# Eighteen of twenty-four down-projection blocks per layer by seven block products

## The chip, the cores and the metric

The kernel runs on one core of a Trainium2 chip. The metric is the device time of one execution in microseconds (us). Three runs of the kernel before took 2449.74, 2450.14 and 2452.28 us; the median, 2450.14 us, is the time that the change is measured against. The engines are named as the profile names them: PE (TensorE, matrix products), PEld (its weight loads), DVE (VectorE), ACT (ScalarE), POOL (GpSimd) and SP (SyncE, which here only issues DMAs).

## The reference, cut to what matters

The model is a two-layer decoder trunk on a sequence of 1024 tokens with 1024 features, in float32. Layer 0 mixes tokens by a gated linear recurrence, layer 1 by stick-breaking attention. After each mixer stands a residual sum with layer normalisation, and then the same channel mixer, which is what the change touches:

```
def conv_ffn(x, w_up, conv_w, conv_b, w_down):
    h = causal_depthwise_conv(x @ w_up, conv_w, conv_b)
    return (jax.nn.gelu(h[..., :D_FF]) * h[..., D_FF:]) @ w_down
...
        x = layer_norm(DN_ALPHA * x + mix, ln_g[layer, 0], ln_b[layer, 0])
        f = conv_ffn(x, ffn_w_up[layer], ffn_conv_w[layer], ffn_conv_b[layer], ffn_w_down[layer])
        x = layer_norm(DN_ALPHA * x + f, ln_g[layer, 1], ln_b[layer, 1])
```

D_FF is 3072: `w_up` is 1024x6144 (gate and value halves), `w_down` is 3072x1024. The convolution looks back two tokens.

## The kernel before

Every float32 matrix product is made of three passes: each operand is split into a rounded high part and the rest (`Split`, line 88, `split_sb`: ACT casts the high part, POOL subtracts it from the source for the low part, line 96), and high x high, high x low and low x high are summed in PSUM. A matmul instruction is 128x128 by 128x512.

The channel mixer of a layer has two phases. The **up phase** (`up`, line 421) goes through 24 blocks j of 128 gate and 128 value channels. Blocks 0, 1 and 23 (`PLAIN`) are done plainly, 96 matmuls each (8 slices of 128 features x 2 halves of tokens x 2 operands x 3 passes). The others go through `seven` (line 533): the 2x2 block product of a weight block (gate and value rows by two halves of features) with x (two halves of features by two halves of tokens) is done by seven products of 12 matmuls instead of eight (the Winograd form of Strassen's rule), so 84 matmuls a block. For this DVE makes four sums of weight blocks per block (`combine`, line 459), and the products add up in three PSUM tiles: `p` for one product, and `cv` and `cg`, whose halves are called c21, c22, c11 and c12. Between the products ACT copies c22 to c11 (line 549) and DVE writes c12 = c22 + p (line 554), which must be done before PE may go on adding into c22 in the product called w3 here (its matmuls read `whi` of sum s3). The sums of x that the seven products need (T1 to T4) are made once per layer, in block 0 (`sums_of_x`, line 488), and live in `Ts`.

When a block's products are done, `activate` (line 481) makes the convolution from PSUM (ACT scales, DVE adds two shifted terms, line 477), ACT applies gelu to the gate, DVE multiplies gate by value (line 485), and SP stores the gated block to DRAM (`gd`, 512 KB). With `ug` and `uv` below the gate's and the value's result are meant.

The **down phase** (`down`, line 571) goes through the 24 gated blocks in eight groups of three. `load` brings the three gated blocks and their weight rows back, ACT and POOL split them (128x1024 each), and `accumulate` (line 141) multiplies: per group 8 tiles of 128 tokens x 2 halves of features x 3 blocks x 3 passes = 144 matmuls for 16 PSUM tiles, each added by DVE to the residual `xres` (line 165, line 161 in the first group). The last two groups run with the layer normalisation (`Finish`).

The order on each engine is set by a scheduler when the program is built: each engine takes its own instructions in a fixed order, and waits at each for what it needs. Where two loops meet, a few instructions of the next block stand between those of the last: PE has four matmuls of the next block between the fourth and the fifth product of a block; they are called fillers here. Buffers come from pools (`bufs=` gives how many of a tile there are): a new tile waits until all readers of the tile that had its buffer are done. The pool `sums` has four buffers for the sums s1 to s4.

## Time and profile before

| | |
|---|---|
| median of three runs | 2450.14 us |
| profiled execution | 2452.94 us, of it the span from first to last instruction 2451.2 us |
| PE busy | 2362.0 us, 96% of the span, 10948 matmuls |
| DVE busy | 1330.6 us, 54% |
| POOL busy | 1122.7 us, 46% |
| ACT busy | 926.3 us, 38% |
| granted TensorE clock, mean | 0.983 of full speed |
| DMA | 71 GB/s over the span |

An engine is busy when one of its instructions runs. Matmuls are pipelined, so that each seems to last 389 ns while a new one starts about every 227 ns; PE's pace is read from starts. The stages are: the recurrence up to about 340 us, the up phase of layer 0 to 843, its down phase to 1107, attention to about 1680, the up phase of layer 1 to 2181 and its down phase to the end.

### The profile page before, as it was taken

The page shows a single profiled execution, that of the slowest core. Times are in us where ns is not written, and L with a number is a line of the kernel's source. Part 1 is how long each engine was busy: PE and PEld are TensorE (multiplying, and loading weights), DVE is VectorE, ACT ScalarE, POOL GpSimd, SP SyncE. Part 2 cuts the span into 40 slices and gives each one's busy share as a digit, 9 for nine tenths or more (in the row PEclk, how much of TensorE's full clock was granted, in tenths as well). Part 3 has the DMA queues.
Part 4 walks back from the last instruction along what each step waited for, and adds up shares of the span by engine and source line. Part 5 has one row for each costly group of instructions (what it writes and reads, how often), then busy time and mean ns, then how long its engine had stood idle before and what let it go on. Part 6 is the DMA issues. An engine that isn't in the chain of part 4 may idle for free. (4 is left out here: it accounts for less than half of the span.)

```text
span 2451.2 us, 28627 instructions
## 1 busy us (share of the span) xinstructions
PE 2362.0 (96%) x10948; PEld 1931.2 (79%) x10948; DVE 1330.6 (54%) x1558; ACT 926.3 (38%) x1379; POOL 1122.7 (46%) x776
## 2 busy tenths in 40 slices
PE   8989979999999999999999999988999999999998
PEld 6877768777777888888877887867877777788887
DVE  5695665555555433362565555585655555533336
ACT  4644234444444411113433343343444444431111
POOL 4686265444444553353332232236544444454444
PEclk9999989999999999998999999999999999999999
DMA  6111111222222433202010110001222222153321
GB/s 216 53 54 52 35 43 57 78 82 78 85 88 69 154 112 88 91 12 69 27 35 27 35 35 32 30 18 61 66 90 78 78 82 79 64 180 104 103 69 69
DMA packets 64072, 176.15 MB, mean 72 GB/s; under 512 B 7104, under 2 KB 8768, under 8 KB 63936
## 3 DMA queue, kind: packets, MB, share of 16 engines
q1 hardware_dynamic: 59328, 160.46, 20.4%
q10 hardware_dynamic: 4608, 13.87, 1.7%
q8 instruction: 86, 1.41, 0.2%
q14 instruction: 50, 0.41, 0.1%
HBM read 144.94 MB, written 29.36 MB: 71 GB/s over the span
## 5 line engine op out<-in xcount | busy, mean ns | idle before, releaser
L96 POOL TENSOR_TENSOR wlo<-wraw,whi 128x512 fp32r<-128x512 f32 (+2 forms) x219 | 366.0, 1681 | 436.8 <-ACT whi L90 422.0
L96 POOL TENSOR_TENSOR wlo<-s,whi 128x512 fp32r<-128x512 f32 x168 | 218.0, 1298 | 250.0 <-ACT whi L90 220.0
L165 DVE TENSOR_TENSOR xres<-xres,po 128x512 f32<-128x512 f32 x264 | 169.6, 681 | 294.8 <-PE po L157 294.5
L153 PE MATMUL po<-dh,mh 128*128 128x512 f32 x768 | 299.3, 390 | 0.0
L154 PE MATMUL po<-dl,mh 128*128 128x512 f32 x768 | 298.8, 389 | 0.0
L90 ACT CAST whi<-wraw 128x512 fp32r<-128x512 f32 (+2 forms) x211 | 147.0, 701 | 288.3 <-PE cv L467 134.1
L157 PE MATMUL po<-dh,ml 128*128 128x512 f32 x768 | 237.3, 389 | 0.0
L96 POOL TENSOR_TENSOR ml<-mraw,mh 128x1024 fp32r<-128x1024 f32 x48 | 115.4, 2405 | 231.3 <-ACT mh L90 219.8
L467 PE MATMUL cv<-Th,whi 128*128 128x512 f32 x504 | 205.4, 408 | 1.6
L90 ACT CAST whi<-s 128x512 fp32r<-128x512 f32 x168 | 104.3, 621 | 271.0 <-PE cg L467 145.4
L467 PE MATMUL cv<-Th,wlo 128*128 128x512 f32 x504 | 196.7, 390 | 0.0
L467 PE MATMUL cv<-Tl,whi 128*128 128x512 f32 x504 | 196.6, 390 | 0.0
L153 PEld LDWEIGHTS po<-dh,mh 128*128 128x128 f32 x768 | 144.1, 188 | 30.6 <-DVE xres L165 0.7
L157 PEld LDWEIGHTS po<-dh,ml 128*128 128x128 f32 x768 | 144.2, 188 | 29.9
L154 PEld LDWEIGHTS po<-dl,mh 128*128 128x128 f32 x768 | 144.2, 188 | 29.6
L459 DVE TENSOR_TENSOR s<-wraw 128x512 f32<-128x512 f32 x84 | 60.5, 720 | 188.8 <-POOL wlo L96 188.4
L90 ACT CAST mh<-mraw 128x1024 fp32r<-128x1024 f32 x48 | 50.4, 1049 | 291.3 <-PE po L154 248.5
L114 PE MATMUL pp<-xTh,whi 128*128 128x512 f32 x352 | 143.4, 407 | 1.6 <-ACT whi L90 1.6
L116 PE MATMUL pp<-xTh,wlo 128*128 128x512 f32 x352 | 137.9, 392 | 0.0
L115 PE MATMUL pp<-xTl,whi 128*128 128x512 f32 x352 | 137.7, 391 | 0.0
L467 PEld LDWEIGHTS cv<-Th,whi 128*128 128x128 f32 x504 | 94.4, 187 | 47.4 <-ACT cg L549 17.6
L467 PE MATMUL cg<-xTh,whi 128*128 128x512 f32 x336 | 130.7, 389 | 0.0
(225 smaller groups left out, 5705.0 us busy)
## 6 DMA issues: line engine op xcount, KB each, us to landing
wraw<-in_w_up SPq DMA_DIRECT2D x192, 256.0 KB, 2.7
gd<-u SPq DMA_DIRECT2D x48, 512.0 KB, 3.1
mraw<-gd SPq DMA_DIRECT2D x48, 512.0 KB, 3.6
draw<-in_w_down SPq DMA_DIRECT2D x48, 512.0 KB, 3.9
wraw<-in_w_in SPq DMA_DIRECT2D x14, 512.0 KB, 3.7
wraw<-in_w_o SPq DMA_DIRECT2D x9, 512.0 KB, 3.6
xres<-in_x ACTq DMA_DIRECT2D x8, 512.0 KB, 5.0
wraw<-in_w_out SPq DMA_DIRECT2D x8, 512.0 KB, 3.7
```

What stands on the lines that cost most here:

```text
L90: A.copy(out=hi, in_=src)
L96: eng.tensor_tensor(out=lo, in0=src, in1=hi.bitcast(F32), op=ALU.subtract)
L114: T.matmul(out, lhsT=l.hi, rhs=r.hi, start=start, stop=False)
L115: T.matmul(out, lhsT=l.hi, rhs=r.lo, start=False, stop=False)
L116: T.matmul(out, lhsT=l.lo, rhs=r.hi, start=False, stop=stop)
L153: T.matmul(po[h], lhsT=g.hi, rhs=w.hi[:, d], start=st, stop=False)
L154: T.matmul(po[h], lhsT=g.hi, rhs=w.lo[:, d], start=False, stop=False)
L157: T.matmul(po[h], lhsT=g.lo, rhs=w.hi[:, d], start=False, stop=sp)
L165: V.tensor_tensor(out=xres[t][:, d], in0=xres[t][:, d], in1=po[h], op=ALU.add)
L459: V.tensor_tensor(out=s, in0=x, in1=y, op=op)
L467: T.matmul(ps, lhsT=l, rhs=r[:, c, :], start=start and c == k == 0, stop=stop and c == 3 and k == 2, skip_group_check=True)
```

## The change

The up phase does block 23 by seven products too (`PLAIN` is now blocks 0 and 1). The gated blocks 0 to 17 are taken in nine pairs. For each pair `store` makes, in the up phase of the block after the pair, the four sums of gated half blocks that a seven-product down-projection needs: four instructions on POOL (lines 513 to 519), in buffers of the pool `sums`, and seven DMAs of 256 KB (line 508) in place of two of 512 KB.

In the down phase a new function, `sevens`, does the nine pairs in three groups. A group goes through the seven products one at a time, each over the three pairs: 12 matmuls per pair, 36 per product, into four PSUM tiles of which each is for one tile of 128 tokens in both halves of the sequence. That makes 252 matmuls for the six blocks that took two groups of 144 before. Each product splits its own operands, six of 128x512 (three gated sums, called `graw` when read back, g when split, and three weights, `wr` or `wt`, w when split): ACT casts the high parts, POOL makes the low parts, from the ninth operand on every third of them DVE. The four sums of weights per pair are made on DVE (line 675), three of the four in place. After a product DVE adds its four tiles to `xres`, once or twice (lines 650 and 653). The last six blocks go as before. The four PSUM banks pairs of the down phase are now called px (four banks) and py0, py1 (two each).

Other edits go with these: the raw weight blocks of the up phase have two pools of four buffers instead of one of eight; block j+1's weights are asked for before block j's work; the fourth sum of x (T4) uses the place of a half of x that is not read later, and is made in block 2 instead of block 0, after the second use of c22; `uv` and `ug` have pools of their own; `gap` keeps a place in SBUF free.

```diff
-        PLAIN = (0, 1, NFF - 1)
+        PLAIN = (0, 1)
...
+        NSEV = NFF - 2 * GROUP
+        GAP = GROUP * HS
+
         def ffn(layer, last):
-            gd = [dram.tile([P, S], F32, name=f"gd{layer}_{j}") for j in range(NFF)]
+
+            gd = [[dram.tile([P, HS], F32, name=f"gs{layer}_{m}_{i}") for i in range(7)] for m in range(NSEV // 2)]
+            gd += [dram.tile([P, S], F32, name=f"gd{layer}_{j}") for j in range(NSEV, NFF)]
...
-                rawp = pool("raw", bufs=8)
+                uw = pool("uw", bufs=1)
+                rawp = [pool(f"raw{i}", bufs=4) for i in range(2)]
                 sums = pool("sums", bufs=4)
+                gap = pool("gap", bufs=1)
                 tq = pool("tq", bufs=1)
+
+                gap.tile([P, GAP], F32, name="gap")
...
-                      for i in range(4)]
+                      for i in range(3)] + [xq[0][1]]
...
+                    done.append(ug)
+
+                done = []
+
+                def store(j):
+
+                    if j >= NSEV:
+                        queue = nc.scalar if j == NFF - 1 else nc.sync
+                        queue.dma_start(out=gd[j - NSEV + NSEV // 2], in_=done[j])
+                    elif j % 2:
+                        a11, a21, a12, a22 = two(done[j - 1]) + two(done[j])
+                        s1, s2, s4 = (sums.tile([P, HS], F32, name="s", tag="s") for _ in range(3))
+
+                        def keep(i, x):
+                            nc.sync.dma_start(out=gd[j // 2][i], in_=x)
+
+                        keep(0, a11)
+                        keep(1, a12)
+                        keep(6, a22)
+                        G.tensor_tensor(out=s1, in0=a21, in1=a22, op=ALU.add)
+                        keep(3, s1)
+                        G.tensor_tensor(out=a21, in0=a11, in1=a21, op=ALU.subtract)
+                        keep(4, a21)
+                        G.tensor_tensor(out=s2, in0=s1, in1=a11, op=ALU.subtract)
+                        keep(2, s2)
+                        G.tensor_tensor(out=s4, in0=a12, in1=s2, op=ALU.subtract)
+                        keep(5, s4)
...
+                        if 3 in which:
+                            ts = [None, t2s.pop(0), None, sums.tile([P, HS], F32, name="s", tag="s")]
+                        else:
+                            ts = [sums.tile([P, HS], F32, name="t2" if i == 1 else "s", tag="t2" if i == 1 else "s")
+                                  for i in range(3)] + [None]
+                            t2s.append(ts[1])
+                        for i, p, q in ((0, y[:, lo_], x[:, lo_]), (2, y[:, hi_], y[:, lo_]),
...
                     product(c22, w2, t2, False, False)
+                    if j == len(PLAIN):
+                        sums_of_x((3,))
                     product(c11, w12, b21, False, True)
                     V.tensor_tensor(out=c12, in0=c22, in1=p5s, op=ALU.add)
                     product(c22, w3, t3, False, True)
...
+                    if j:
+                        store(j - 1)
                     activate(j, *ps)
+                store(NFF - 1)
...
+        def sevens(layer, gd, ph, banks):
+            def pool(name, **kw):
+                return ph.enter_context(tc.tile_pool(name=f"{name}_s{layer}", reuse_waits="tile", **kw))
+            wtp = pool("wt", bufs=5)
+            wrps = [None, pool("wr1", bufs=14), pool("wr0", bufs=12)]
+            wrps[0] = wrps.pop()
+            rawp = pool("graw", bufs=4)
+            wfp = pool("wf", bufs=GROUP)
+            ring = pool("ring", bufs=6)
+            def operand(src, name):
+                w = Split(ring.tile([P, HS], F32R, name=name + "h", tag=name + "h"),
+                          ring.tile([P, HS], F32R, name=name + "l", tag=name + "l"))
+                turns[0] += 1
+                split_sb(w.hi, w.lo, src, lo_eng="dve" if turns[0] > 8 and turns[0] % 3 == 0 else "pool")
+                return w
+            turns = [0]
+            seen = set()
+            def add(t, h, ps):
+                x = xres[t][:, HALVES[h]]
+                if (t, h) in seen:
+                    V.tensor_tensor(out=x, in0=x, in1=ps, op=ALU.add)
+                else:
+                    seen.add((t, h))
+                    V.scalar_tensor_tensor(out=x, in0=x, scalar=ALPHA, in1=ps, op0=ALU.mult, op1=ALU.add)
+            for group, m0 in enumerate(range(0, NSEV // 2, GROUP)):
+                B = {}
+                wrp = wrps[group % 2]
+                def weight(n, m):
+                    def w(n):
+                        return weight(n, m)
+                    if (n, m) in B:
+                        return B[n, m]
+                    if n in ("11", "12", "21", "22"):
+                        k, d = int(n[0]) - 1, HALVES[int(n[1]) - 1]
+                        out = (wfp if n == "11" else wrp).tile([P, HS], F32, name="wr", tag="wr")
+                        nc.sync.dma_start(out=out, in_=a["w_down"][layer, (2 * m + k) * P:(2 * m + k + 1) * P, d])
+                    else:
+                        x, y, place = {"T1": ("12", "11", "11"), "T2": ("22", "T1", None), "T3": ("22", "12", "12"),
+                                       "T4": ("21", "T2", "21")}[n]
+                        x, y = w(x), w(y)
+                        out = w(place) if place else wtp.tile([P, HS], F32, name="wt", tag="wt")
+                        V.tensor_tensor(out=out, in0=x, in1=y, op=ALU.subtract)
+                    B[n, m] = out
+                    return out
+                for n in ("11", "21"):
+                    for m in range(m0, m0 + GROUP):
+                        weight(n, m)
+                acc = [None, None]
+                for i, n, c, on, into in ((0, "11", 0, False, ((0, 0),)), (1, "21", 1, False, ((0, 0),)),
+                                          (2, "T2", 0, True, ((0, 1),)), (3, "T1", 1, False, ((1, 1),)),
+                                          (4, "T3", 0, True, ((1, 0), (1, 1))), (5, "22", 1, True, ((0, 1),)),
+                                          (6, "T4", 0, False, ((1, 0),))):
+                    if not on:
+                        acc[c] = [banks[(group + c) % 2].tile([P, HS], F32, name="po", tag="sm") for _ in range(4)]
+                    for m in range(m0, m0 + GROUP):
+                        raw = rawp.tile([P, HS], F32, name="graw", tag="graw")
+                        nc.sync.dma_start(out=raw, in_=gd[m][i])
+                        g = operand(raw, "g")
+                        w = operand(weight(n, m), "w")
+                        for t in range(4):
+                            gt = g[:, t * P:(t + 1) * P]
+                            for k, (l, r) in enumerate(((gt.hi, w.hi), (gt.hi, w.lo), (gt.lo, w.hi))):
+                                T.matmul(acc[c][t], lhsT=l, rhs=r, start=not on and m == m0 and k == 0,
+                                         stop=m == m0 + GROUP - 1 and k == 2, skip_group_check=True)
+                    for t in range(4):
+                        for th, h in into:
+                            add(4 * th + t, h, acc[c][t])
...
+                pends = [pool(f"py{i}", bufs=2, space=PSUM) for i in range(1)]
+                pmid = pool("px", bufs=4, space=PSUM)
+                pends.append(pool("py1", bufs=2, space=PSUM))
+
+                class Ends:
+
+
+                    n = 0
+
+                    def tile(self, *args, **kw):
+                        self.n += 1
+                        return pends[(self.n + 1) // 2 % 2].tile(*args, **kw)
+
+                pend = Ends()
+                with ExitStack() as ph7:
+                    sevens(layer, gd, ph7, (pmid, pend))
...
-                for k in range(NG - 2):
-                    gs, ws = load(k)
-                    accumulate(pb, gs, ws, first=(k == 0))
```

On the engines the change moves instructions at three places. The names carry the program's numbers; the numbers differ between the two programs.

Up phase, DVE, from the gate-times-value product of one block (L485, now L493) to the addition c12 = c22 + p of the next (L554, now L598). Before:

```order
L485 TENSOR_TENSOR u_3178<-u_3178,u_3183 128x1024
L459 TENSOR_TENSOR s_3493<-wraw_3487,wraw_3489 128x512
L554 TENSOR_TENSOR cg_3259<-cv_3233,p5s_3261 128x512
L459 TENSOR_TENSOR s_3495<-s_3493,wraw_3485 128x512
L558 TENSOR_TENSOR cv_3233<-cv_3233,p5s_3261 128x512
```

Now, in the block after a pair:

```order
L485 SCALAR_TENSOR_TENSOR uv_3560<-cv_3462,pv_66,uv_3560 128x1022
L493 TENSOR_TENSOR ug_3555<-ug_3555,uv_3560 128x1024
L467 TENSOR_TENSOR s_3734<-wraw_3567,wraw_3569 128x512
L467 TENSOR_TENSOR s_3736<-s_3734,wraw_3565 128x512
L598 TENSOR_TENSOR cg_3635<-cv_3609,p5s_3637 128x512
L467 TENSOR_TENSOR s_3738<-wraw_3565,wraw_3567 128x512
```

Two sums of the next block's weights stand ahead of the addition instead of one; the second, s_3736, has the buffer of the pair's first gated sum, s_3702 (the pool goes round in four). In the block after that one the addition follows the product directly.

The same place on POOL, after the change (before, there are only instructions of line 96 there):

```order
L96 TENSOR_TENSOR wlo_3743<-wraw_3565,whi_3742 128x512
L513 TENSOR_TENSOR s_3702<-ug_3408,ug_3555 128x512
L515 TENSOR_TENSOR ug_3408<-ug_3408 128x512
L517 TENSOR_TENSOR s_3703<-s_3702,ug_3408 128x512
L519 TENSOR_TENSOR s_3704<-ug_3555,s_3703 128x512
L96 TENSOR_TENSOR wlo_3747<-s_3734,whi_3746 128x512
```

Four sums of gated blocks have moved in ahead of the low part of s_3734; the last reader of s_3702 on POOL is the third of them, and its reader beside POOL is the DMA gs0_2_3 of line 508.

End of the up phase, DVE, from the last block's last addition into c22 (L558 of block 22 before, L602 of block 23 now). Before:

```order
L485 TENSOR_TENSOR u_5990<-u_5990,u_5995 128x1024
L477 SCALAR_TENSOR_TENSOR u_6123<-pg_6026,pv_66,u_6123 128x1023
L477 SCALAR_TENSOR_TENSOR u_6123<-pg_6026,pv_66,u_6123 128x1022
L477 SCALAR_TENSOR_TENSOR u_6128<-pu_6025,pv_66,u_6128 128x1023
L477 SCALAR_TENSOR_TENSOR u_6128<-pu_6025,pv_66,u_6128 128x1022
L161 SCALAR_TENSOR_TENSOR xres0_75<-xres0_75,po_6196 128x512
```

Now:

```order
L602 TENSOR_TENSOR cv_6202<-cv_6202,p5s_6230 128x512
L675 TENSOR_TENSOR wr_6344<-wr_6512,wr_6344 128x512
L675 TENSOR_TENSOR wr_6512<-wr_6510,wr_6512 128x512
L675 TENSOR_TENSOR wr_6346<-wr_6541,wr_6346 128x512
L675 TENSOR_TENSOR wr_6541<-wr_6539,wr_6541 128x512
L485 SCALAR_TENSOR_TENSOR ug_6296<-cg_6228,pv_66,ug_6296 128x1023
L675 TENSOR_TENSOR wt_6515<-wr_6510,wr_6344 128x512
L485 SCALAR_TENSOR_TENSOR ug_6296<-cg_6228,pv_66,ug_6296 128x1022
```

Five sums of down weights have come in ahead of and between the last gate convolution, which frees the PSUM bank that PE's first down matmul writes. Those sums write in place of weights that POOL reads (wl_6367 reads wr_6344, wl_6389 reads wr_6346):

```order
L96 TENSOR_TENSOR gl_6363<-graw_6360,gh_6362 128x512
L96 TENSOR_TENSOR wl_6367<-wr_6344,wh_6366 128x512
L96 TENSOR_TENSOR gl_6385<-graw_6382,gh_6384 128x512
L96 TENSOR_TENSOR wl_6389<-wr_6346,wh_6388 128x512
L96 TENSOR_TENSOR gl_6407<-graw_6404,gh_6406 128x512
L96 TENSOR_TENSOR wl_6411<-wr_6348,wh_6410 128x512
L96 TENSOR_TENSOR gl_6437<-graw_6434,gh_6436 128x512
L96 TENSOR_TENSOR wl_6441<-wr_6350,wh_6440 128x512
```

PE's first down matmuls, right behind block 23, now read gh_6436 with wh_6440 and wl_6441, that is what the seventh and eighth of these instructions write:

```order
L475 MATMUL cv_6202<-xTh01_85,wlo_6199 128x512
L699 MATMUL po_6430<-wh_6440,gh_6436 128x512
L699 MATMUL po_6430<-wl_6441,gh_6436 128x512
L699 MATMUL po_6430<-wh_6440,gl_6437 128x512
```

What moved there: the second product's first tiles stand ahead of the first product; before, the down phase began with the first tile of its first group behind 96 matmuls of block 23.

## Rows read from the trace of the kernel before

**Rows 1.** Stretches: up and down phase, layer 1; length, busy (count) by engine, PEclk.

```profile
1749.00:2151.00 402.00, 401.23 (x1729) 320.99 (x1727) 224.54 (x220) 182.32 (x268) 185.79 (x144) 1.00 0.24 80
2181.00:2443.00 262.00, 261.93 (x1156) 216.56 (x1154) 106.18 (x153) 50.17 (x49) 125.62 (x62) 1.00 0.29 93
```

**Rows 2.** PE's timeline at the start and end of layer 0's down phase.

```profile
842.64 0.61 PE L127 MATMUL pu<-xTh,wlo 128*128 128x512 f32 x2
843.09 0.39 PE L153 MATMUL po<-dh,mh 128*128 128x512 f32 x1
...
1079.73 0.49 PE L230 MATMUL pt<-ident,xres 128*128 128x128 f32 x3
```

**Rows 3.** PE's groups from 843.0 to 1080.0 us.

```profile
L153 PE MATMUL po<-dh,mh 128*128 128x512 f32 x348 | 135.4, 389 | 0.0
```

**Rows 4.** PE's timeline in a block that began at 2101.6: third and fifth product.

```profile
2105.91 0.39 PE L467 MATMUL p<-Th,wlo 128*128 128x512 f32 x1
2106.35 0.50 PE L467 MATMUL cv<-Th,whi 128*128 128x512 f32 x1
...
2112.63 0.39 PE L467 MATMUL cv<-xTh,whi 128*128 128x512 f32 x1
2112.90 0.50 PE L467 MATMUL cv<-Th,whi 128*128 128x512 f32 x1
```

**Rows 5.** DVE's timeline in the same block.

```profile
2101.55 2.60 DVE L477 SCALAR_TENSOR_TENSOR u<-cg,pv,u 128x1023 f32<-128x1023 f32 x2
...
2104.66 2.59 DVE L477 SCALAR_TENSOR_TENSOR u<-cv,pv,u 128x1023 f32<-128x1023 f32 x2
2107.36 2.16 DVE L485 TENSOR_TENSOR u<-u 128x1024 f32<-128x1024 f32 x1
2111.28 0.69 DVE L459 TENSOR_TENSOR s<-wraw 128x512 f32<-128x512 f32 x1 [1.76 <-POOL wlo L96]
2112.15 0.70 DVE L554 TENSOR_TENSOR cg<-cv,p5s 128x512 f32<-128x512 f32 x1 [0.17 <-PE cg L467]
```

**Rows 6.** ACT's timeline in the same block.

```profile
2099.44 1.20 ACT L475 ACTIVATE u<-cg,pv 128x1024 f32<-128x1024 f32 x1
2102.16 1.21 ACT L475 ACTIVATE u<-cv,pv 128x1024 f32<-128x1024 f32 x1
2115.78 0.62 ACT L90 CAST whi<-wraw 128x512 fp32r<-128x512 f32 x1 [3.18 <-PE cv L467]
2116.30 0.58 ACT L557 COPY cv<-cv 128x512 f32<-128x512 f32 x1
```

**Rows 7.** POOL's timeline: four low parts in a row, and two around 398 us.

```profile
359.02 5.02 POOL L96 TENSOR_TENSOR wlo<-wraw,whi 128x512 fp32r<-128x512 f32 x4
...
396.65 2.97 POOL L96 TENSOR_TENSOR wlo<-s,whi 128x512 fp32r<-128x512 f32 x2
```

**Rows 8.** DVE's timeline at 398.4 and 415.3 us.

```profile
398.41 1.76 DVE L459 TENSOR_TENSOR s<-wraw 128x512 f32<-128x512 f32 x1 [0.57 <-POOL wlo L96]
...
415.34 1.23 DVE L485 TENSOR_TENSOR u<-u 128x1024 f32<-128x1024 f32 x1
```

**Rows 9.** The page, DMA issues: KB each, median us from issue to landing.

```profile
wraw<-in_w_up SPq DMA_DIRECT2D x192, 256.0 KB, 2.7
```

**Rows 10.** PE's timeline: first matmul after an idle time (in brackets).

```profile
1395.25 0.62 PE L114 MATMUL pu<-whi,oh 128*128 128x512 f32 x1 [1.80 <-DVE xres L716]
1600.70 0.48 PE L778 MATMUL po<-wth,vh 128*128 128x128 f32 x1 [2.58 <-ACT wth L639]
```

**Rows 11.** Stretches behind such idle times; the third number from the end is PEclk.

```profile
1327.90:1331.30 3.40, 3.06 (x15) 2.31 (x15) 3.40 (x5) 1.15 (x3) 0.45 (x2) 1.00 0.33 135
1395.30:1398.70 3.40, 3.40 (x10) 2.97 (x11) 3.34 (x4) 0.56 (x3) 0.00 (x0) 0.53 0.38 145
1600.80:1604.20 3.40, 3.40 (x10) 2.91 (x11) 2.65 (x6) 1.00 (x3) 0.58 (x2) 0.50 0.00 0
```

**Rows 12.** The page, DVE's additions from PSUM to the residual.

```profile
L165 DVE TENSOR_TENSOR xres<-xres,po 128x512 f32<-128x512 f32 x264 | 169.6, 681 | 294.8 <-PE po L157 294.5
```

More of the change, by code (lines that the diff above doesn't have):

```diff
@@ L452, in blocks @@
                     for f, k in ((0, 0), (1, 0), (1, 1), (0, 1)):
[L453 removed]
+                        raw = out[f, k] = rawp[j % 2].tile([P, HS], F32, name="wraw", tag="wraw")
                         nc.sync.dma_start(out=raw, in_=a["w_up"][layer, f * NFF + j][:, k * HS:(k + 1) * HS])
@@ L481, in activate, with sums_of_x @@
                 def activate(j, pg, pu):
-                    ug = conv(pg, j)
+                    ug = conv(pg, j, "ug", 2)
                     A.activation(out=ug, in_=ug, func=AF.Gelu_apprx_tanh)
-                    uv = conv(pu, NFF + j)
+                    uv = conv(pu, NFF + j, "uv", 1)
                     V.tensor_tensor(out=ug, in0=ug, in1=uv, op=ALU.mult)
-                    nc.sync.dma_start(out=gd[j], in_=ug)
-                def sums_of_x():
+                    done.append(ug)
[20 more added lines that the diff above has]
+                        keep(5, s4)
+                t2s = []
+                def sums_of_x(which):
                     for t in ((0, 1, 2, 3) if not last else (0, 1, 3, 2)):
@@ L492, in sums_of_x @@
                         lo_, hi_ = slice(0, HS), slice(HS, D)
-                        ts = [sums.tile([P, HS], F32, name="s", tag="s") for _ in range(4)]
-                        for o, p, q in ((ts[0], y[:, lo_], x[:, lo_]), (ts[2], y[:, hi_], y[:, lo_]),
-                                        (ts[1], y[:, hi_], ts[0]), (ts[3], x[:, hi_], ts[1])):
-                            G.tensor_tensor(out=o, in0=p, in1=q, op=ALU.subtract)
-                        for i in (0, 2, 1, 3):
+                        if 3 in which:
[5 more added lines that the diff above has]
+                        for i, p, q in ((0, y[:, lo_], x[:, lo_]), (2, y[:, hi_], y[:, lo_]),
+                                        (1, y[:, hi_], ts[0]), (3, x[:, hi_], ts[1])):
+                            if i in which:
+                                G.tensor_tensor(out=ts[i], in0=p, in1=q, op=ALU.subtract)
+                        for i in which:
                             pt = pp5.tile([P, HS], F32, name="pt", tag="p5")
@@ L516, in __getitem__, with plain @@
                         return self.k[k][:, c:c + P]
-                def plain(j, order):
-                    a11, a12, a21, a22 = (operand(r) for r in blocks(j))
+                def plain(j, raws, order):
+                    a11, a12, a21, a22 = (operand(r) for r in raws)
                     pu = pcv.tile([P, S], F32, name="pu", tag="cv")
@@ L531, in plain, with seven @@
                     return pg, pu
-                def seven(j):
-                    r11, r12, r21, r22 = blocks(j)
+                def seven(j, raws):
+                    r11, r12, r21, r22 = raws
                     (b11, b12), (b21, b22) = xq
@@ L560, in seven @@
                     return cg, cv
+                nxt = blocks(0)
                 for j in range(NFF):
+                    raws, nxt = nxt, blocks(j + 1) if j + 1 < NFF else None
                     if j in PLAIN:
-                        ps = plain(j, None if j else PAIRS if last else (0, 1, 2, 3))
-                    else:
-                        ps = seven(j)
-                    if j == 0:
-                        sums_of_x()
+                        ps = plain(j, raws, None if j else PAIRS if last else (0, 1, 2, 3))
+                        if j == 0:
+                            sums_of_x((0, 2, 1))
+                    else:
+                        ps = seven(j, raws)
+                    if j:
+                        store(j - 1)
@@ L593, in load @@
                     for j in range(k * GROUP, (k + 1) * GROUP):
-                        out[0].append(block(gd[j], "m", k % 2))
+                        out[0].append(block(gd[j - NSEV + NSEV // 2], "m", k % 2))
                         out[1].append(block(a["w_down"][layer, j * P:(j + 1) * P, :], "d", k % 2))
@@ L608, in after @@
                     else:
-                        transpose_x(psm, t)
+                        transpose_x(pmid, t)
                 gs, ws = load(NG - 2)
                 e = range(4)
-                accumulate(pb, gs, ws, False, tiles=e)
+                accumulate(pend, gs, ws, False, tiles=e)
                 g2, w2 = load(NG - 1)
-                Finish(psm, gs + g2, ws + w2, gb, after, early=(GROUP, e), lag=0 if last else 4,
+                Finish(pmid, gs + g2, ws + w2, gb, after, early=(GROUP, e), lag=0 if last else 4,
                        fast=2 if last else 0).run(range(NT))
```

14 lines of the change are left out of this document (5 added, 9 removed).

## The prediction, made before the changed kernel was run

> **What bounds the kernel now.** I read the stretches by stage first. In the up and in the down phase alike PE is busy from end to end at a granted clock of 1.00, while DVE, ACT and POOL are busy for about half of the time or less [rows 1]. So the time goes with the number of matmuls times PE's pace. The pace comes from starts on PE's timeline: layer 0's down phase has its first matmul at 843.09 and its last before 1079.73, 348 of each of three kinds, 1044 in all [rows 2, 3]: 236.64 / 1044 = 0.2267 us each. The up phase starts 1729 matmuls in 402 us, 0.2325 each [rows 1], so that a block of 84 takes 19.53 us where 84 x 0.2267 is 19.04: 0.49 us of PE's time are lost per block. The timeline of one block shows where: the third product starts 0.44 after the matmul before it, the fifth 0.27, both with slow first matmuls [rows 4]. The fifth follows DVE's addition c12 = c22 + p, which ends at 2112.85 [rows 5], 0.05 before. That addition is the place to watch. Between the two phases PE has no gap: block 23's last matmuls (two from 842.64) run into the first down matmul at 843.09 [rows 2].
>
> **What goes.** Six groups of 144 matmuls become three of 252, 108 fewer per layer, and block 23 needs 84 where it had 96. That is 120 per layer, 240 in all: 240 x 0.2267 = **54.4 us less**, if nothing new makes PE wait. The rest is what new waits cost.
>
> **The block after a pair (16 times).** Times here are from the start E of that block's PE work; 2101.6 is E in the rows. After the change DVE takes, in order: gate convolution, value convolution, gate times value, s_3734, s_3736, then the addition. The value's scaling on ACT ends at E + 1.8 [rows 6], the two shifted terms take 2.6 [rows 5]: E + 4.4. The product needs two inputs from SBUF, and such DVE work does not run beside POOL: at 415.34 it took 1.23 alone, at 2107.36 2.16 beside POOL; a sum at 398.41 took 1.76, as it first stood out the POOL instruction that ended at 399.62 and then needed 0.55 [rows 5, 7, 8]. I take the end of the product at E + 5.8 (0.3 of waiting, 1.1 of work). Then POOL has the low part wlo_3743 (a pitch of 1.255 [rows 7], about 1.16 after waiting) to 7.0, DVE s_3734 0.55 to 7.5, POOL the first gated sum s_3702 to 8.7, the second to 9.9, the third to 11.2. s_3736 waits for two things, as it takes the buffer of s_3702: for the third gated sum, and for the DMA that stores s_3702, issued at 8.7; at the 2.7 us that a 256 KB load needs from issue to landing [rows 9] it lands at 11.4. POOL's fourth gated sum starts at 11.2, s_3736 stands it out to 12.4, ends at 12.95, and the addition behind it takes 0.70 [rows 5]: the fifth product can start at E + 13.7. PE arrives there after 8 + 12 + 12 + 12 matmuls of the block and 5 fillers, 49 x 0.2267 = E + 11.1. **Stall: 2.6 us.** Bounds: if s_3736 goes ahead of the fourth sum, 1.6; if everything on POOL is as short as it can be and the store lands early, 0.3 (the third sum no later than the fillers); with the 1.49 us that two low parts took each at 396.65 [rows 7] for POOL's five, 3.6. I take 2.6, since POOL's next instruction needs no message from another engine to start. 16 x 2.6 = 41.6.
>
> The Trainium skill, page "SBUF — State Buffer", section "SBUF: two separate sides", says that of a GpSimd instruction and a VectorE instruction with two SBUF inputs, whichever starts first holds the shared ports for the whole instruction. The sum at 398.41 agrees, with 1.21 us of waiting inside its 1.76 [rows 8]. By that rule the fourth gated sum goes first and the stall is 2.6, without the rule it would be 1.6.
>
> In the other blocks the addition follows the product of gate and value with no sum between, and the ACT copy that the third product waits for comes earlier with the convolutions; I leave them 0.1 each of the 0.49. There are 44 blocks by sevens now, so 28 x 0.1 = 2.8, while the 42 x 0.49 = 20.6 of before go. The up phases: 41.6 + 2.8 - 20.6 = **+23.8 us**.
>
> **The clock.** Five idle times of 1.80 us before a matmul stand at 1260 to 1531; behind three of them the granted clock is 0.53 to 0.65 for the next 3.4 us, behind two it is 1.00. Behind each of four of 2.05 to 2.87 us it is 0.50 to 0.57 [rows 10, 11]; these are falls to the lower of the two levels for part of the stretch. A fall to 0.56 over 3.4 us costs 1.5 us. A stall of 2.6 shows as an idle time of 2.4 (a matmul lasts 0.39 where the pitch is 0.23), between the two kinds: I take 10 of 16, **+15 us** (bounds 0 and 24).
>
> **The start of the down phase (twice).** PE's first down matmuls need wl_6441, the eighth low part on POOL. ACT can cast for these only after its copy of c22 to c21, which follows the fifth product: a copy of 0.58 and a cast of 0.62 [rows 6]. Behind the fifth product PE has 24 matmuls, 5.4 us, so POOL starts 4.1 us before block 23 ends. Eight at 1.255 are 10.0: ready 5.9 us after the end. Up to four sums of weights on DVE come between, which shut POOL out for 0.55 each: 8.1. On DVE the third and fourth of these sums, waiting for POOL's fourth low part, stand ahead of the gate convolution (1.3 twice, another sum between), which frees the first PSUM bank: 6 to 8 us after the end as well. I take 7.0, and a fall of the clock behind it (1.5): 2 x 8.5 = **+17 us**. Bounds 2 x 5.9 and 2 x 10. Before, block 23's 96 plain matmuls needed only four operands, and hid all of it.
>
> **Down phase.** A product has 36 matmuls, 8.16 us. Of its six operands about four low parts are on POOL, 4 x 1.255 = 5.0, and two on DVE; with 12 sums per group these exclude each other: 28 x 1.255 + 26 x 0.55 = 49 us of a group's 57.1 on PE. Hidden. DVE also adds four or eight tiles per product at 0.68 [rows 12], which need not wait for POOL. But at a group's end seven sums of the next group's weights and a low part stand ahead of the additions that free the banks for the next group's second product: eight times 0.55 to 1.8 against 8.16 less four additions, 5.4. I take 1.0 us at each of four places, **+4 us** (0 to 5 each). The four T4 sums in block 2 put four ACT copies and four DVE subtractions ahead of its addition: 1.0 per layer, **+2 us** (0 to 1.5 each).
>
> **Sum.** -54.4 + 23.8 + 15 + 17 + 4 + 2 = +7.4. The profiled execution took 2452.94, the median of the runs is 2.8 below it: 2460.3 there, **2457 us** as the runs are counted.
>
> **Rivals.** Against less than 0.2% (5 us) a measurement of this kernel cannot tell a change.
> 1. The buffer is free in time. If POOL and the store are done by E + 10.5, the stall is 0.3 at most: 16 x 0.3 + 2.8 - 20.6 = -13.0, no falls of the clock but at the starts: -54.4 - 13.0 + 17 + 4 + 2 = -44.4, so **2406**. For it: POOL is 54% idle over the span. Against it: five POOL instructions behind a product that ends no earlier than E + 5.6.
> 2. DVE goes ahead of POOL's fourth sum, or the chain runs a microsecond sooner: stall 1.6, 25.6 + 2.8 - 20.6 = 7.8; the idle time is then 1.4, shorter than any behind which the clock fell in the rows; I leave 7 for some. -54.4 + 7.8 + 7 + 23 = -16.6: **2434**, faster. It decides once the stall is below about 2.0.
> 3. The clock falls in every pair and the starts are at their upper end: 23.8 + 24 + 20 + 8 + 3 - 54.4 = +24.4: **2475**. For it: all idle times over 2 us in the rows.
> 4. POOL becomes the bound of the down groups. With 1.48 per low part, as around 398 us, and 0.69 per sum, 28 x 1.48 + 26 x 0.69 = 59.4 against 57.1: 2.3 x 6 = +14 on the forecast, **2472**. Against it: most low parts took 1.30.
>
> That the matmuls do not go is no rival: the order of the changed program has 756 in the seven-product part of a layer's down phase.
>
> **How the numbers follow.** Forecast 0.35 (its own range 2445 to 2471; of it 0.05 within 0.2%); rival 1 0.18, rival 2 0.26 (of it 0.05 within), rival 3 0.13, rival 4 0.08. Faster: 0.18 + 0.21 + 0.01 = 0.40; same 0.10; slower 0.50. The range 2408 to 2480 leaves out the lower half of rival 1 and the upper part of rivals 3 and 4.
>
> **What would show it.** In the block after each pair: PE's idle time ahead of the fifth product, with DVE's addition as its releaser, and the second sum ahead of that waiting for POOL or for a DMA; 16 of them of 2.4 us make the forecast, under 1.5 rival 2. Behind them, PEclk. One idle time of 6 to 8 us per layer at the start of the down phase, released by POOL or DVE. Down groups of 57 us each, or 59 and more (rival 4). It is wrong in kind if the blocks after pairs are no longer than the others, or if a wait decides that is not named here, such as the read-back of the gated sums.

## The result: slower by 0.9%

The changed kernel takes 2473.53 us (median of four runs, 2469.09 to 2474.16), the kernel before 2450.57 in the same series: a ratio of 1.0089, 95% interval 1.0071 to 1.0106. The forecast was 2457 with a range of 2408 to 2480.

The page of the changed kernel, its span, busy times and the counts of its matmuls:

```profile
span 2471.4 us, 29325 instructions
PE 2306.7 (93%) x10708; PEld 1886.2 (76%) x10708; DVE 1533.0 (62%) x1722; ACT 1004.3 (41%) x1571; POOL 1334.2 (54%) x954
```

PE has its 240 matmuls less and 55 us less of busy time; the span is 20 us longer all the same. The stretches show where [rows 1] (length, then busy time and count of PE, PEld, DVE, ACT and POOL, PEclk, share of DMA, GB/s). Up phase of layer 1, the idle time ahead of layer 0's down phase, what follows it, and a part of the down phase:

```profile
1755.00:2211.00 456.00, 430.39 (x1861) 345.85 (x1859) 262.79 (x241) 196.79 (x290) 261.18 (x190) 1.00 0.28 96
863.70:873.20 9.50, 0.11 (x2) 0.04 (x1) 9.43 (x8) 3.25 (x7) 9.50 (x7) 0.73 0.28 84
873.20:878.30 5.10, 5.10 (x12) 4.08 (x13) 5.10 (x7) 1.50 (x2) 1.02 (x1) 0.50 0.31 104
883.00:940.00 57.00, 57.00 (x253) 47.22 (x252) 40.34 (x51) 25.07 (x44) 41.62 (x31) 1.00 0.54 171
```

In layer 1 the 402 us of up phase in [rows 1] had 0.8 us without PE; the 456 us of now have 26. Before the down phase PE stands for 9.5 us while DVE and POOL are busy all the time, and then runs at half clock. Within a down group PE is busy from end to end (57.00 of 57.00 us): the seven products themselves are as fast as hoped.

PE's timeline in the block after a pair (the idle time and its releaser in brackets): fifth and seventh product of the block, then the start of the down phase and the end of its first group.

```profile
463.49 0.50 PE L475 MATMUL cv<-Th,whi 128*128 128x512 f32 x1 [1.37 <-DVE cg L598]
...
470.76 0.50 PE L475 MATMUL cv<-xTh,whi 128*128 128x512 f32 x1 [1.54 <-DVE cv L602]
...
873.19 0.77 PE L699 MATMUL po<-wh,gh 128*128 128x512 f32 x1 [9.39 <-DVE ug L485]
...
942.25 0.47 PE L699 MATMUL po<-wh,gh 128*128 128x512 f32 x1 [1.10 <-DVE xres L650]
```

Before, PE lost some 0.05 us at the first place [rows 4] and nothing at the second, where the seventh product of that block starts 0.23 us after the matmul before it:

```profile
2118.25 0.39 PE L467 MATMUL cg<-xTh,wlo 128*128 128x512 f32 x1
2118.48 0.39 PE L467 MATMUL cv<-Th,whi 128*128 128x512 f32 x1
```

DVE's timeline in the block after a pair, to be laid beside [rows 5]:

```profile
455.33 1.31 DVE L493 TENSOR_TENSOR ug<-ug,uv 128x1024 f32<-128x1024 f32 x1
456.56 1.77 DVE L467 TENSOR_TENSOR s<-wraw 128x512 f32<-128x512 f32 x1
462.13 0.69 DVE L467 TENSOR_TENSOR s<-s,wraw 128x512 f32<-128x512 f32 x1 [3.79 <-POOL s L517]
462.74 0.69 DVE L598 TENSOR_TENSOR cg<-cv,p5s 128x512 f32<-128x512 f32 x1
465.24 1.76 DVE L467 TENSOR_TENSOR s<-wraw 128x512 f32<-128x512 f32 x1 [1.80 <-POOL wlo L96]
466.92 0.68 DVE L467 TENSOR_TENSOR s<-wraw,s 128x512 f32<-128x512 f32 x1
467.52 1.77 DVE L467 TENSOR_TENSOR s<-wraw 128x512 f32<-128x512 f32 x1
469.40 0.69 DVE L467 TENSOR_TENSOR s<-s,wraw 128x512 f32<-128x512 f32 x1
470.01 0.69 DVE L602 TENSOR_TENSOR cv<-cv,p5s 128x512 f32<-128x512 f32 x1
```

The second sum stands idle for 3.79 us until POOL's third gated sum is done; the addition of line 598 is queued behind it, as forecast. Then four more sums, of which the first waited 1.80 us for a low part of POOL and two stood out a POOL instruction, are queued ahead of the addition of line 602, which the seventh product waits for. That second wait is in no case of the prediction. POOL at the same time:

```profile
460.81 1.29 POOL L517 TENSOR_TENSOR s<-s,ug 128x512 f32<-128x512 f32 x1
462.18 1.77 POOL L519 TENSOR_TENSOR s<-ug,s 128x512 f32<-128x512 f32 x1
```

The fourth gated sum took 1.77: DVE's sum, at 462.13, went first and POOL stood it out, the other way than forecast. So it is in fifteen of the sixteen blocks in which PE waits for the addition of line 598. In the sixteenth the order was the forecast's. DVE's sum was released by the DMA that stores the pair's first gated sum and started 0.5 us after the end of POOL's third sum; POOL's fourth had started, and the sum stood it out. DVE, POOL and PE there:

```profile
2101.87 1.39 DVE L467 TENSOR_TENSOR s<-s,wraw 128x512 f32<-128x512 f32 x1 [4.26 <-DMA gs<-s]
2101.45 1.26 POOL L519 TENSOR_TENSOR s<-ug,s 128x512 f32<-128x512 f32 x1
2103.93 0.80 PE L475 MATMUL cv<-Th,whi 128*128 128x512 f32 x1 [2.53 <-DVE cg L598]
```

PE's idle time was 2.53 us there, the clock fell behind it, and the seventh product did not wait.

At the start of the down phase, DVE and then POOL:

```profile
862.16 6.79 DVE L675 TENSOR_TENSOR wr<-wr 128x512 f32<-128x512 f32 x4 [2.46 <-POOL wl L96]
868.88 1.27 DVE L485 SCALAR_TENSOR_TENSOR ug<-cg,pv,ug 128x1023 f32<-128x1023 f32 x1
870.07 1.78 DVE L675 TENSOR_TENSOR wt<-wr 128x512 f32<-128x512 f32 x1
871.77 1.27 DVE L485 SCALAR_TENSOR_TENSOR ug<-cg,pv,ug 128x1022 f32<-128x1022 f32 x1
863.35 1.71 POOL L96 TENSOR_TENSOR wl<-wr,wh 128x512 fp32r<-128x512 f32 x1
```

The first down matmul starts when the gate convolution has ended, behind five sums of weights.

### The profile page after: what moved, and what is told of

Same layout as the page of the kernel before. It is cut to its first block, busy times and chain, and to the rows that moved or that the text cites. A ratio compares the mean times of both kernels' runs of the same rounds, so it can differ in the third digit from the quotient of the medians.

```text
span 2471.4 us, 29325 instructions
## 1 busy us (share of the span) xinstructions
PE 2306.7 (93%) x10708; PEld 1886.2 (76%) x10708; DVE 1533.0 (62%) x1722; ACT 1004.3 (41%) x1571; POOL 1334.2 (54%) x954
## 4 chain that ended last, share of the span: by engine, by line
PE 56%; DVE 11%; issue 10%; POOL 6%; ACT 1%; DMA 0%; POOLq 0%; DVEq 0%; ACTq 0%
PE cv L475 16%; PE po L699 11%; PE cg L475 5%; PE p L475 5%; DVE s L467 2%; PE pp L114 2%; DVE e L891 2%; PE pp L115 2%; PE pp L116 2%; PE po L153 2%; PE po L154 2%; PE po L157 2%; DVE wr L675 1%; DVE xres L862 1%; POOL s L513 1%
## 5 line engine op out<-in xcount | busy, mean ns | idle before, releaser
L699 PE MATMUL po<-wh,gh 128*128 128x512 f32 x504 | 198.3, 395 | 23.2 <-DVE ug L485 18.8
L699 PE MATMUL po<-wl,gh 128*128 128x512 f32 x504 | 198.0, 393 | 0.0
L699 PE MATMUL po<-wh,gl 128*128 128x512 f32 x504 | 198.0, 393 | 0.0
L96 POOL TENSOR_TENSOR gl<-graw,gh 128x512 fp32r<-128x512 f32 x86 | 123.9, 1443 | 111.9 <-ACT gh L90 103.7
L475 PE MATMUL cv<-xTh,whi 128*128 128x512 f32 x352 | 139.0, 395 | 25.7 <-DVE cv L602 25.7
L90 ACT CAST gh<-graw 128x512 fp32r<-128x512 f32 x126 | 78.4, 622 | 190.5 <-PE po L699 68.4
L485 DVE SCALAR_TENSOR_TENSOR ug<-cg,pv,ug 128x1023 f32<-128x1023 f32 x88 | 112.6, 1280 | 49.3 <-ACT ug L483 47.8
L475 PE MATMUL cg<-xTh,wlo 128*128 128x512 f32 x352 | 137.1, 390 | 0.0
L475 PE MATMUL cv<-xTl,whi 128*128 128x512 f32 x352 | 137.1, 389 | 0.0
L475 PE MATMUL cg<-xTl,whi 128*128 128x512 f32 x352 | 137.0, 389 | 0.0
```

The source lines that it names most:

```text
L90: A.copy(out=hi, in_=src)
L96: eng.tensor_tensor(out=lo, in0=src, in1=hi.bitcast(F32), op=ALU.subtract)
L475: T.matmul(ps, lhsT=l, rhs=r[:, c, :], start=start and c == k == 0, stop=stop and c == 3 and k == 2, skip_group_check=True)
L485: V.scalar_tensor_tensor(out=u[:, k:], in0=ps[:, :S - k], scalar=cw[:, 2 - k:3 - k], in1=u[:, k:], op0=ALU.mult, op1=ALU.add)
L699: T.matmul(acc[c][t], lhsT=l, rhs=r, start=not on and m == m0 and k == 0, stop=m == m0 + GROUP - 1 and k == 2, skip_group_check=True)
```

## The experiments

Ten kernels ran. Times are medians, ratios are to the kernel before with their 95% interval.

**Buffers of their own for the gated sums.**

```diff
-                gap = pool("gap", bufs=1)
+                gap = pool("gap", bufs=GROUP)
...
-                gap.tile([P, GAP], F32, name="gap")
...
-                        s1, s2, s4 = (sums.tile([P, HS], F32, name="s", tag="s") for _ in range(3))
+                        s1, s2, s4 = (gap.tile([P, HS], F32, name="gs", tag="gs") for _ in range(3))
```

> The changed kernel, but the gated sums s1, s2 and s4 of line 505 have three buffers of their own (in the place that the tile gap kept free) instead of three of the pool sums. Same instructions, same DMAs; DVE's order in the block after a pair is then that of before, with one weight sum ahead of the addition c12 = c22 + p and one between it and c22 = c22 + p. Theory A (the two waits in each block after a pair, 1.53 and 1.71 us, come from the shared buffers and from the sums that are queued ahead of the two additions because of them): a pair of blocks goes from 41.84 us back to about 39.1, 16 x 2.8 = 44 us less, about 2429 us; no idle time over 1 us ahead of the fifth and seventh product. Rival B (the waits come from POOL's four added sums per pair, which shut DVE out): the pairs stay near 41.8 us, time about 2465 to 2475.

Measured: 2552.7 us, 1.042 (1.0403 to 1.0437): 79 us slower than the changed kernel, where 44 less were expected. DVE's and POOL's timelines in the block after a pair (lines are one less than in the changed kernel):

```profile
462.38 1.73 DVE L466 TENSOR_TENSOR s<-wraw 128x512 f32<-128x512 f32 x1 [6.58 <-POOL wlo L96]
464.03 0.69 DVE L597 TENSOR_TENSOR cg<-cv,p5s 128x512 f32<-128x512 f32 x1
```

```profile
455.88 1.29 POOL L512 TENSOR_TENSOR gs<-ug 128x512 f32<-128x512 f32 x1 [1.16 <-DVE ug L492]
457.25 1.29 POOL L514 TENSOR_TENSOR ug<-ug 128x512 f32<-128x512 f32 x1
458.50 1.28 POOL L516 TENSOR_TENSOR gs<-gs,ug 128x512 f32<-128x512 f32 x1
459.86 1.26 POOL L518 TENSOR_TENSOR gs<-ug,gs 128x512 f32<-128x512 f32 x1
461.08 2.48 POOL L96 TENSOR_TENSOR wlo<-s,whi 128x512 fp32r<-128x512 f32 x2
```

With a ring of four for weight sums alone DVE runs on into the sums of the block after next. The one sum ahead of the addition now needs the buffer of the next block's first sum, which POOL reads (wlo at 461.08) only behind all four gated sums. So the same queue waits for the end of POOL's four instead of for the third, and for longer: 5.5 us of idle PE in each of sixteen blocks, with a slow clock behind each of them. The order that reads like that of before was no proof that nothing in it waits. Theory A as worded, that shared buffers make the wait, is wrong.

**The same with the addition ahead of that sum.** `tc.issue_after(x)` queues what is written in its block behind instruction x on x's engine; `adds[0]` is the addition c12 = c22 + p of the block before, `adds[1]` its c22 = c22 + p.

```diff
-                    s1 = combine(ALU.add, r21, r22)
+                    s1 = combine(ALU.add, r21, r22, adds[0])
```

> e1_own_buffers with one change of order: a block's first sum of weights is queued on DVE behind the addition c12 = c22 + p of the block before. In e1 the addition stood behind such a sum (s_3880), whose buffer comes free with a low part that POOL makes only behind the four gated sums. Theory A1 (what counts is that nothing that waits for POOL stands ahead of the addition; whose the buffers are doesn't matter): the idle time of 5.9 us per pair goes, time within 6 us of e14_sums_behind_adds, 2413 to 2425. Rival H (buffers of their own cost something else, such as the place in SBUF or the stores): stays above 2440.

Measured: 2425.18, 0.9893 (0.9879 to 0.9906). 127 us come back for one place in a queue. It is 6.6 us above e14, just outside what was expected: its up phases take 433.6 and 434.1 us where e14's (the run after next) take 430.8. The trace shows where: the third and fourth sum stand ahead of the addition c22 = c22 + p as before, and in fifteen blocks the seventh product waits for that addition, some 0.55 us each. In e14, which queues these sums behind it, no such wait is left.

```profile
464.18 0.50 PE L477 MATMUL cv<-xTh,whi 128*128 128x512 f32 x1 [0.57 <-DVE cv L604]
```

**No gated sums at all.** This kernel leaves POOL's four sums out and stores unsummed half blocks, as many bytes as before, so its values are not the reference's.

```diff
-                        G.tensor_tensor(out=s1, in0=a21, in1=a22, op=ALU.add)
...
+                        for i, x in ((0, a11), (1, a12), (6, a22), (3, a22), (4, a21), (2, a11), (5, a12)):
+                            keep(i, x)
```

> The changed kernel with the gated sums left out: POOL's four instructions per pair (lines 513 to 519) are gone, and the seven DMAs store unsummed half blocks, as many bytes as before. Theory A: DVE's order in the up phase is again that of before, and nothing waits for POOL's sums; the time is that of e1_own_buffers within 4 us, since in e1 POOL's sums lie beside other work. Rival B: well below e1 (by 10 us and more), as POOL's sums cost DVE time wherever their buffers lie.

Measured: 2426.61, 0.99 (0.9886 to 0.9915). Without POOL's sums the stalls of the up phase are gone. The stretch 410 to 820 in this run and then in the kernel before, columns as above:

```profile
410.00:820.00 410.00, 408.84 (x1768) 327.02 (x1767) 235.08 (x233) 185.21 (x273) 189.03 (x147) 1.00 0.28 97
410.00:820.00 410.00, 408.69 (x1761) 327.20 (x1761) 225.34 (x222) 185.07 (x271) 188.42 (x146) 1.00 0.25 84
```

But e19 has all the sums and the same time: so it is not POOL's work that costs, but who waits for it.

**Only DVE's order in the up phase.** Buffers and POOL's order are those of the changed kernel.

```diff
-                    s2 = combine(ALU.subtract, s1, r11)
-                    s3 = combine(ALU.subtract, r11, r21)
-                    s4 = combine(ALU.subtract, r12, s2)
+                    s2 = combine(ALU.subtract, s1, r11, adds[0])
+                    s3 = combine(ALU.subtract, r11, r21, adds[1])
+                    s4 = combine(ALU.subtract, r12, s2, adds[1])
```

> The changed kernel with only DVE's queue in the up phase changed: a block's second sum of weights is queued behind the addition c12 = c22 + p of the block before, its third and fourth behind c22 = c22 + p. Buffers, instructions and POOL's order are those of the changed kernel. Theory A1 (the two waits of a pair are a matter of what stands ahead of the two additions in DVE's queue): pairs go from 41.84 to about 39.3 us, no wait over 0.3 us ahead of the fifth and seventh product, 16 x 2.6 = 41 us less: about 2432. Rival A2 (POOL's four sums per pair are too much work at that place; if the additions don't wait, the operands of the next block do): PE waits elsewhere, pairs stay above 41 us, time above 2462.

Measured: 2418.6, 0.9865 (0.9851 to 0.988): 55 us below the changed kernel (41 were expected) and 33 below the kernel before. DVE's timeline in the block after a pair:

```profile
454.92 1.77 DVE L468 TENSOR_TENSOR s<-wraw 128x512 f32<-128x512 f32 x1
459.45 0.70 DVE L601 TENSOR_TENSOR cg<-cv,p5s 128x512 f32<-128x512 f32 x1 [2.77 <-PE cg L478]
460.49 0.69 DVE L468 TENSOR_TENSOR s<-s,wraw 128x512 f32<-128x512 f32 x1 [0.34 <-POOL s L520]
464.26 0.70 DVE L605 TENSOR_TENSOR cv<-cv,p5s 128x512 f32<-128x512 f32 x1 [3.08 <-ACT cv L604]
```

And its stretch 410 to 820, with the columns of the stretches above:

```profile
410.00:820.00 410.00, 409.31 (x1779) 329.95 (x1778) 236.67 (x235) 188.07 (x276) 258.54 (x184) 1.00 0.28 99
```

Both additions now wait for PE and ACT, that is for their own inputs, and the sum that waits for POOL does so behind them. POOL has all its work (258.54 us in the stretch) and PE is busy for 409.31 of 410 us. One wait over 0.4 us is left in each up phase, 0.86 ahead of the fifth product of block 23, which the changed kernel has too. Theory A1 holds, rival A2 falls.

**Block 23 plain again**, on the changed kernel and on e1. Block 23 then reads T4 where a half of x stood before, so its values are not the reference's; the work is.

```diff
-        PLAIN = (0, 1)
+        PLAIN = (0, 1, NFF - 1)
```

> As e1_own_buffers, and block 23 plain again, 96 matmuls in place of 84. Theory A for the start of the down phase (the idle time of 9.55 us and the slow clock behind it are there because POOL can begin on the first operands only 4 us before block 23 ends, and four weight sums on DVE stand ahead of the last gate convolution): the idle time goes to under 1 us, each layer gains 9.55 + 2.5 for the clock and pays 12 x 0.2267 = 2.7, so 2 x 9.3 = 19 us less than e1, about 2410. Rival C (the first operands are late whatever block 23 is, since the read-back from DRAM or the weight sums' alternation with POOL sets it): an idle time of several us stays, and the run is no more than 8 us faster than e1, or slower by up to 5.

> The changed kernel with only block 23 plain again; the gated sums stay in the pool sums. Theory A: the pairs keep 41.84 us, the start of the down phase has no idle time over 1 us: 19 us less than the changed kernel, about 2454. Rival C: 2466 to 2478.

Measured: 2532.29 on e1, 20.4 less, as expected. On the changed kernel 2476.05, where 2454 were expected. There too the idle time ahead of the down phase is gone: its first matmul (line 699) starts 0.23 us after the last of block 23.

```profile
879.63 0.62 PE L127 MATMUL pu<-xTh,wlo 128*128 128x512 f32 x2
880.09 0.39 PE L699 MATMUL po<-wh,gh 128*128 128x512 f32 x1
```

And block 23 with the down phase takes 263.9 us in layer 0 where the changed kernel needs 19.0 + 9.8 + 244.7 = 273.5. But the edit moved the schedule of the first pairs, too:

```profile
425.34 0.79 PE L475 MATMUL cv<-Th,whi 128*128 128x512 f32 x1 [4.55 <-DVE cg L598]
```

21 seven-product blocks take 449.8 us, where 22 took 456.1 in the changed kernel: 13 us lost per layer. What stands in the trace for the start is as theory A has it; the sum of the run alone would have spoken for rival C.

**The order at the start of the down phase.** `ends["conv"]` is the last block's convolution, `ends["mm"]` the last matmul of the first product; `behind` is `tc.issue_after`. The first group's sums of weights now stand behind the one, its second product behind the other.

```diff
+                        with behind(ends["conv"] if group == 0 else None):
                             V.tensor_tensor(out=out, in0=x, in1=y, op=ALU.subtract)
...
+                                with behind(ends["mm"] if group == 0 and i == 1 else None):
+                                    mm = T.matmul(acc[c][t], lhsT=l, rhs=r, start=not on and m == m0 and k == 0,
...
```

> The changed kernel with only the order at the start of the down phase changed: the first group's second product is queued on PE behind its first, and the first group's sums of weights on DVE behind the last block's convolution. Theory D (the 9.55 us and the slow clock behind them come from PE beginning with a product whose operands are the seventh and eighth on POOL and whose bank waits for the convolution; the first product needs POOL's first two and banks that are free): idle time under 1 us, no slow clock, 2 x 12 = 24 us less: about 2449. Rival E (POOL and ACT are late with any first operand, since they begin only behind the fifth product of block 23): 4 us and more of idle time stay, 2458 or more.

> Both changes of order together (e14_sums_behind_adds and e16_start_order). If the two costs are independent, as theories A1 and D have it: 2473.5 - 41 - 24, about 2408, faster than the kernel before by 42 us. If one hides behind the other: above 2420.

Measured: 2469.09 alone (1.0072, 1.0057 to 1.0087), and with e14's order 2418.89, no less than e14 without it (2418.6). In e16 PE goes from block 23 into the first product without a gap (0.23 us from start to start). Then it stands ahead of the third product:

```profile
887.50 0.76 PE L710 MATMUL po<-wh,gh 128*128 128x512 f32 x1 [8.74 <-DVE xres L662]
```

The idle time of 9.39 has become one of 8.74, two products later. Theory D named the right two queues and was wrong on the time, since it asked only what is late at the first matmul.

**Group ends, and the first group's later sums.** e17 queues the second and third group's sums behind the last addition of the group before; e18 also queues the six sums that the third product doesn't need behind the first product's additions (`ends["add0"]`). The line of e18 against that of e16:

```diff
-                        with behind(ends["conv"] if group == 0 else None):
+                        with behind(ends["add"] if group else ends["conv"] if n in ("T1", "T2") else ends["add0"]):
```

> As e15_both_orders, and the sums of weights of the second and third group are queued on DVE behind the last addition of the group before. Theory F (the 1.26 us of waiting at each of four group ends come from the seven sums queued ahead of the additions that free the banks): none left, 5 us less than e15, about 2403. Rival G (moved back, the sums are late for the third product, which needs them): the same as e15 or up to 8 us more.

> As e17_also_group_ends, and of the first group's twelve sums of weights the six that the third product doesn't need are queued on DVE behind the additions of the first product (in e17 the third product's first matmul waits 8.7 us for these additions, which stand behind eleven sums). Theory I (the wait is the queue on DVE): six sums of 1.7 us are gone from ahead of the additions, the idle time falls from 8.7 to about 4 us, 2 x 4.5 less: about 2405. Rival J (DVE and POOL together have too much work that excludes the other one in the first 25 us of a down phase, whatever its order): the idle time moves on to a later product, or stays, and the time is that of e17 within 3 us.

Measured: e17 2413.73 (0.9845, 0.983 to 0.9859), 5.2 us below e15 with no wait left at the group ends: theory F. e18 2411.24 (0.9837, 0.9824 to 0.985), 2.5 below e17, within the 3 us of rival J. DVE's timeline in e17 suggests why the idle time was not ordered away, and a stretch of it shows DVE and POOL busy for 24.91 and 23.44 of 25 us:

```profile
842.34 3.48 DVE L686 TENSOR_TENSOR wr<-wr 128x512 f32<-128x512 f32 x2
845.74 2.37 DVE L686 TENSOR_TENSOR wt<-wr 128x512 f32<-128x512 f32 x2
...
855.38 3.42 DVE L686 TENSOR_TENSOR wr<-wr,wt 128x512 f32<-128x512 f32 x2
858.72 2.46 DVE L662 SCALAR_TENSOR_TENSOR xres<-xres,po 128x512 f32<-128x512 f32 x4
...
834.00:859.00 25.00, 16.80 (x75) 13.57 (x73) 24.91 (x19) 11.69 (x20) 23.44 (x16) 0.90 0.51 168
```

Beside POOL's low parts a sum takes up to 1.7 us where it needs 0.6, and POOL's part up to 1.7 where it needs 1.25. In e18 PE waits twice instead of once, for ACT and for an addition; 2.1 and 3.7 us in layer 0, 2.1 and 5.3 in layer 1. Layer 0's:

```profile
PE po L711 <- DVE xres L659: 3.7, 1, 3.7
PE po L711 <- ACT gh L90: 2.1, 1, 2.1
```

So the greater part stays, and moves. That POOL and ACT begin only 4 us before block 23 ends and have, with DVE, more to do for the first three products than PE has, is argued from these rows; a start with earlier operands was not tried. e18 is the fastest version, 40 us below the kernel before.

## Why the prediction was right in sign, and where its terms were not

By its own steps, in the profiled executions (span 2451.2 before, 2471.4 now, +20.2 where the sum gave +7.4):

- **Matmuls gone**: 240, -54.4 as worked out.
- **Up phases.** Forecast +23.8, with the clock's 15 and T4's 2: +40.8. Measured: 456.1 + 457.1 where 432.8 + 432.8 stood, +47.7, and 12 x 2 matmuls fewer in them, so +53.1. The mechanism was right: DVE's addition behind a sum that waits for POOL's third gated sum. The addition ended at E + 12.6, E being 450.85. The step that failed is "I take 2.6, since POOL's next instruction needs no message from another engine to start": in fifteen of sixteen blocks DVE went first, and the wait was 1.53 as in rival 2 (1.76 from start to start, less 0.23). Only in the block at 2103.93, where the store landed last, did the forecast's order and its idle time come. What made up for it is the wait of 1.71 ahead of the seventh product, from the same queue (the third to sixth sum), which I never followed past the first addition. Together 3.24 in such a block. Also there are nine pairs per layer, not eight: the first one's sums fall in block 2, which waits once. And the other blocks kept half of their 0.49 us (19.31 for 19.04).
- **The clock.** +15 for 10 falls: one fall in sixteen blocks after pairs. This is the term that was most too large; the idle times were 1.4 and 1.5, not 2.4. Where one of 2.53 stood, at 2103.93, the clock did fall.
- **Luck.** The first wait and the clock were forecast at 41.6 + 15 and cost some 27 (fifteen times 1.53, once 2.7, one fall at the forecast's 1.5). The second wait, fifteen times 1.71 or 26 us, is in no term. That the two together come near the forecast is luck, and so is the sign: the second wait alone is about as much as the whole loss (20.2 us, or 28.8 without the two stretches under "Not forecast"). By the prediction's own test, a wait that decides and is not named there, it was wrong in kind here.
- **Start of the down phase.** Forecast 2 x 8.5. Measured 9.55 of idle time and 5.1 us at PEclk 0.50, 2.5: 12.1 each, +24. Four sums ahead of the convolution took 6.79 us where I had 4 x 0.55 beside POOL's parts: each stood out a POOL instruction.
- **Group ends**: 1.26 each, +5 for a forecast of +4. **Down groups** run at PE's pace: rival 4 falls.
- **Not forecast**: the stretch from the end of layer 0's down phase to the up phase of layer 1 is 5.8 us shorter, and the up phase of layer 0 starts 2.8 earlier. The second goes with T4's sums, which left block 0; right behind layer 0's down phase there were 13.7 us at half clock before and 3.4 now. Which part of that is the change's own isn't settled.

Of the Trainium skill's page "SBUF — State Buffer", section "SBUF: two separate sides", the rule held in kind: one engine stands the other out for a whole instruction (1.77 at 462.18 and 456.56). It does not say which of the two starts first; that the fourth gated sum does was my assumption, and does not follow from the rule as the prediction has it.

Rival 1 (the buffer is free in time) did not come: POOL's third sum ended at E + 11.25, and in e14 the sum still waits 0.34 us for it, but behind the addition, where PE does not feel it. Rival 2 is what happened to the first wait, though not to the time.

## What to carry to other kernels

An engine takes its queue in order: before moving work onto another engine, list what stands in the queue behind the instruction that will wait for it, and follow the queue past the first victim. When a wait is removed, ask what the same engines must have done for the next three steps; if they are short of time as a whole, the wait may only move, as it did at the start of the down phase. And look at waits in the trace, not at the order of the names: e1 had the order of before and waited longest.

## What the runs showed of the hardware

DVE instructions with two inputs from SBUF and POOL instructions took turns in these rows when both had work: a sum of 0.55 to 0.69 us took 1.7 beside POOL (four in 6.79), a POOL part of 1.25 took 1.71. So two engines can be nearly full together although they do not look it: in e17 DVE and POOL are busy 62% and 56% of the span, and 24.91 and 23.44 of the 25 us from 834 on.

In the up phases of the changed kernel the clock stayed at 1.00 behind all 32 of PE's idle times of 1.2 to 1.6 us; behind the one of 2.5 us it fell to 0.50 for a part of what followed, and so it did in e1 behind all sixteen of 5.5 us.
